# Laying out the order of a decoder layer's token mixers on five engines by a list of events with operation times

## The chip, the core and the metric

The kernel runs on one core of a Trainium2 chip. A core has five engines that each work through a list of their own, in its order: TensorE (PE in the profile; PEld is its loading of weights), VectorE (DVE), ScalarE (ACT), GpSimd (POOL) and SyncE (SP, which here only issues DMAs). [...] The metric is the device time of the whole program in microseconds (us), the median of several runs; less is better.

## The reference

The program computes one layer for 512 positions of 2048 channels, in float32. What matters here:

```python
h = rms_norm(x, pre_gain[l]) * (1.0 + scale) + shift      # scale, shift, gate from c
proj = h @ w_in[l]                                        # 97 column tiles of 128
y_a = rwkv7_mix(pa, ...)                                  # r, k, v, a low-rank w and a
y_a = (y_a * jax.nn.silu(z_a)) @ p_a[l]
y_b = (short_conv_mix(pb, conv_w[l]) * jax.nn.silu(z_b)) @ p_b[l]
m = jax.nn.sigmoid(g_a) * y_a + jax.nn.sigmoid(g_b) * y_b
o = m @ w_out[l]
x = x + gate * rms_norm(o, post_gain[l])
```

`rwkv7_mix` holds a recurrence over the positions for 16 heads of 64 channels (`S = S*w + sa*b + v*k`, `y = S@r`), followed by a normalisation of y in each head. `short_conv_mix` is a convolution of width 3 along the positions.

## The kernel before, in words

Every float32 product is made of three matmuls: a weight tile `w` is cut into `H` (a rounded copy, made by ACT) and `L = w - H` (made by POOL; `split`, lines 151 to 153), and the inputs likewise; then H·H, H·L and L·H are added in PSUM (`three`, lines 163 to 166). One column tile of the input projection is 16 blocks deep and so takes 48 matmuls of 128x512. Its weights come in four quarters of 256 KB (`quarter`, line 155: a DMA to `raw`, then `wH` on ACT and `wL` on POOL, four buffers of each).

The program has three stages. The first normalises x, makes the modulation and begins the projection (tiles `firsts`). The second, which the change is about, is the mixers' stage. The third multiplies by `p_b`, `p_a` and `w_out`.

In the mixers' stage PE has two kinds of work. One is the **dense stream**: 83 column tiles `ps_c` (79 whole ones, 4 of half depth), 3888 matmuls of 128x512 in all, each tile evicted from one of two PSUM banks (`mm`) by a function of its own (`use_rkv`, `use_za`, `use_gate` and the four of the convolution). The other is the recurrence, worked out for eight pairs of heads in chunks of 64 positions, by three generators a pair:

- `prepare` (line 523): the operands AR and BK of a pair, with its decays, from the tiles of r, k and v; mostly DVE.
- `invert` (line 629): the triangular matrices of all chunks (`pg`, `GG`), then their inversion on DVE, 62 short operations one after another (`invt`, `Xg`, lines 667 and 669), between DMAs that rearrange the blocks.
- `chunks` (line 708): transposes (`pt`, `pv`, `pz`) and then the **chain** of eight chunks. In each, PE makes `p1 = GK·VB + AR·S` (lines 753 and 755), ACT copies it to `UB` in two halves (757), PE makes `p2 = Kt·VB + S + Z·UB` (760, 762, 764), and ACT copies that to the next state `SB` in two halves (767). `p1` and `p2` hold four chunks in one bank each; `p2` has one bank alone (`py=1` in BANKS). After four chunks their sum goes to `yt`: ACT copies p1 (771) and DVE adds p2 (772). At a pair's end DVE normalises yt and writes it to a block-diagonal `YB` (788), PE turns it back with 8 products by `twoid` (793), ACT scales it (795), POOL adds the bonus (796), DVE gates it (801).

What sets the order: for PE alone it is written out. `drive` (line 177) takes the dense stream three matmuls at a time (`STEP = 0.66`) and goes to a generator when the wait that it last asked for (`WAIT`, in us, lines 34 and 35) has gone by on a clock that `drive` counts up. ACT, DVE, POOL and SP are ordered by the framework's scheduler, by priorities (`URGENT` for the chain) and its own estimates.

Of the kernel before, what the change touches and what calls it, by code (L numbers as in the profile page):

```python
# [8 lines left out]
F32 = mybir.dt.float32  # L9
# [7 lines left out]
P = 128  # L17
# [59 lines left out]
def trunk(ctx: ExitStack, tc: tile.TileContext, xT_d, x_d, prm_d, crow_d, ada1_d, ada2_d, rows_d, w_d, lora_d, pa_d, pb_d,  # L77
# [47 lines left out]

    twoid = cst.tile([P, C], F32, name="twoid")
    V.tensor_copy(twoid[0:C, :], ident[0:C, 0:C])
    V.tensor_copy(twoid[C:P, :], ident[C:P, C:P])
# [48 lines left out]
    def drive(stream, sides):  # L177

        now = 0.0
        with tc.manual_schedule(engines={mybir.EngineType.PE}):
            while stream or sides:
                for sd in list(sides):
                    while sd in sides and sd[1] <= now:
                        try:
                            with tc.high_priority(offset=sd[2]):
                                cost, wait = next(sd[0])
                        except StopIteration:
                            sides.remove(sd)  # L190
                            break
                        if cost == wait == 0:
                            break
                        now += cost
                        sd[1] = now + wait
                if stream:
                    try:
                        next(stream)
                    except StopIteration:
                        stream = None  # L200
                now += STEP

# [21 lines left out]
    hold = {}  # L224

    def use_cg(i, ps):
        cg = ev.tile([P, T], F32, tag="cv", bufs=1, name=f"cg{i}")
        A.activation(cg, ps, AF.Copy)
        hold["cg", i] = cg

    def use_hb(i, ps):
        u = ev.tile([P, T], F32, tag="u", bufs=1, name=f"u{i}")
        V.tensor_tensor(u, ps, hold.pop(("cg", i)), ALU.mult)
        v = ev.tile([P, T], F32, tag="cv", bufs=1, name=f"cv{i}")
        A.activation(v, u, AF.Copy, scale=pc("cw", 16 + i))
# [12 lines left out]
    USES = ((T_CG, use_cg), (T_HB, use_hb), (T_BG, use_bg), (T_ZB, use_zb))
# [224 lines left out]
    with tc.tile_pool(name="rp", bufs=1) as rp:  # L473
# [7 lines left out]
        def within(ps, w, H, L):  # L481

            TE.matmul(ps, w, H, start=True, stop=False)
            TE.matmul(ps, w, L, start=False, stop=True)

        def lerp(dst, ps, i):

            m = ev.tile([P, T], F32, tag="th", bufs=1, name=f"lm{i}")
            A.activation(m, ps, AF.Copy, scale=pc("mu", i))
            V.scalar_tensor_tensor(dst[:, 1:T], ps[:, 1:T], omu[:, i:i + 1], m[:, 0:T - 1], ALU.mult, ALU.add)  # L490
            V.tensor_scalar(dst[:, 0:1], ps[:, 0:1], omu[:, i:i + 1], None, ALU.mult)
# [3 lines left out]
        G.memset(keep, 1.0)  # L495
        G.memset(keep[:, :, 0:1], 0.0)


        la = tmp("la")
        lerp(la, first[T_LORA], T_LORA)  # L500
        A.activation(la[0:HS, :], la[0:HS, :], AF.Tanh)
        twin = tmp("twin")
        S.dma_start(twin[HS:P, :], la[0:HS, :])
        S.dma_start(twin[0:HS, :], la[HS:P, :])
# [4 lines left out]
        halves = (slice(0, HS), slice(HS, P))  # L509
        for i, b in enumerate(halves):  # L510
            A.activation(laH[i][b, :], la[b, :], AF.Copy)
            G.tensor_tensor(laL[b, :], la[b, :], laH[i][b, :].bitcast(F32), ALU.subtract)
            A.activation(wz[halves[1 - i], i], ident[halves[1 - i], :], AF.Copy, scale=0.0)
            A.activation(laH[i][halves[1 - i], :], twin[halves[1 - i], :], AF.Copy)
# [5 lines left out]
        def small(name):  # L520
            return bank("sm", f"ps_{name}")

        def prepare(j, got, out):

            n = f"_{j}"
            wa = rp.tile([P, 2, P], F32R, tag="wa", name="wa" + n)
            raw = tmp("raw" + n).rearrange("p (a b c) -> p a b c", a=2, b=2)
            S.dma_start(raw[:, 0], lora_d[j])
            for i, b in enumerate(halves):
                o = halves[1 - i]  # L530
                A.activation(wa[b, i], raw[b, 0, i], AF.Copy)
                A.activation(wz[b, i], raw[b, 0, i], AF.Copy)
                A.activation(raw[o, 1, i].bitcast(F32R), raw[o, 0, i], AF.Copy)
                G.tensor_tensor(wa[o, i], raw[o, 0, i], raw[o, 1, i], ALU.subtract)
            yield 0, WAIT["w"]
            psw = small("w" + n)
            lowrank(psw, wa[:, 0], 0)
            lw = tmp("lw" + n)
            A.activation(lw, psw, AF.Tanh, bias=hw0[:, j:j + 1], scale=0.5)
            V.tensor_scalar(lw, lw, -0.5 * DECAY, -0.5 * DECAY, ALU.mult, ALU.add)  # L540
            cum3 = c3(lw)
            for t0 in range(0, T, T // 4):
                part = lw[:, t0:t0 + T // 4]
                V.tensor_tensor_scan(part, keep.rearrange("p c t -> p (c t)"), part, 0.0, ALU.mult, ALU.add)
            dec = rp.tile([P, NC, C + 1], F32, tag="dec", name="dec" + n)
            G.memset(dec[:, :, 0:1], 1.0)
            A.activation(dec[:, :, 1:C + 1], cum3, AF.Exp)
            A.activation(lw, lw, AF.Exp, scale=-1.0)
            end = rp.tile([P, NC], F32, tag="end", bufs=2, name="end" + n)
            A.activation(end.unsqueeze(2), dec[:, :, C:C + 1], AF.Copy)  # L550
            yield 0.5, WAIT["a"]
            psa = small("a" + n)
            lowrank(psa, wa[:, 1], 1)
            a = tmp("a" + n)
            A.activation(a, psa, AF.Tanh, bias=hw0[:, 8 + j:9 + j], scale=0.5)
            V.tensor_scalar(a, a, 0.5, 0.5, ALU.mult, ALU.add)
            while "k" not in got:
                yield 0, 0
            kr = got["k"]
            sq = tmp("sq" + n)  # L560
            A.activation(sq, kr, AF.Square, scale=pc("kk", j))
            sH, sL = tmp("sH" + n, F32R), tmp("sL" + n, F32R)
            split(sH, sL, sq)
            yield 0.5, WAIT["k"]

            psk = small("k" + n)
            within(psk, hsumr, sH, sL)
            V.tensor_scalar(sq, psk, 1e-24, None, ALU.max)
            kk = tmp("kk" + n)
            rsqrt(kk, sq, tmp("ku" + n))  # L570
            V.scalar_tensor_tensor(kk, kr, pc("kk", j), kk, ALU.mult, ALU.mult)
            u = tmp("u" + n)
            G.tensor_scalar(u, a, pc("ka", j), oka[:, j:j + 1], ALU.mult, ALU.add)
            V.tensor_tensor(kr, kr, u, ALU.mult)
            yield 0.5, WAIT["kk"]
            while "r" not in got or at["chain"] < j - 1:
                yield 0, 0
            rr, vv = got["r"], got["v"]


            AR = rp.tile([P, NC, P], F32, tag="AR", bufs=2, name="AR" + n)
            BK = blocks_of(j)
            V.tensor_tensor(a, kk, a, ALU.mult)
            for h, b in enumerate(halves):
# [564 lines left out]
```

## Time and profile before

| what | before |
|---|---|
| median of 3 runs (lowest, highest) | 1716.77 us (1715.26, 1724.05) |
| the profiled execution's own time | 1715.66 us |
| its span, first to last instruction | 1713.9 us |
| mean granted TensorE clock | 0.980 |
| PE busy in the span | 1631.9 us, 95% |
| DVE, ACT, POOL busy | 51%, 38%, 47% |
| first and last dense matmul of the mixers' stage | 192.9 us, 1327.1 us |
| DMA, mean | 138 GB/s |

The profile is of one execution. "Busy" of PE counts a matmul from its start to a modelled end, and matmuls overlap; a gap in it is a true wait, though, and the tables of waits name the instruction that waited, what ended the wait and how long it took. The granted clock is the share of full speed that the throttle allowed TensorE; at 0.5 each matmul takes twice as long.

### The profile page before, as it was taken

How to read it: one execution, taken by the hardware profiler on the slowest of the kernel's cores; microseconds unless marked ns; L12 is line 12 of the kernel's file. 1: busy time of each engine (PE TensorE's matmuls, PEld its weight loads, DVE VectorE, ACT ScalarE, POOL GpSimd, SP SyncE). 2: the span in 40 equal slices, each digit the busy share in tenths (PEclk: the TensorE clock that was granted, in tenths of full speed). 3: DMA queues.
4: the chain of work that ended last, by engine and by line, in shares of the span. 5: the costliest groups of instructions: out<-in, count | busy, mean ns of one | idle time of the engine just before them, and what ended most of it. 6: DMA issues, size and time to landing. Idle time of an engine off the chain costs nothing. (4 is left out here: it accounts for less than half of the span.)

```text
span 1713.9 us, 22888 instructions
## 1 busy us (share of the span) xinstructions
PE 1631.9 (95%) x8120; PEld 1345.5 (79%) x8120; DVE 875.3 (51%) x1582; ACT 644.0 (38%) x1331; POOL 805.0 (47%) x649
## 2 busy tenths in 40 slices
PE   6999989999998999998999989999999899999997
PEld 3788877787887887887878878878887687888886
DVE  4997778319629438448168076152002344544405
ACT  4554522344353343443433433433432323232411
POOL 2699653533533534444435434334344344774421
PEclk8999999999999999999999999999999899999999
DMA  8985332323332432322323324343333676665704
GB/s 321 363 330 203 108 103 74 114 78 97 90 90 64 123 83 79 108 83 85 121 84 104 98 75 122 92 119 113 97 105 102 228 240 209 195 197 182 242 32 148
DMA packets 138885, 235.71 MB, mean 138 GB/s; under 512 B 34833, under 2 KB 43665, under 8 KB 134673
## 3 DMA queue, kind: packets, MB, share of 16 engines
q1 hardware_dynamic: 138624, 234.15, 43.3%
q8 instruction: 64, 1.05, 0.2%
q14 instruction: 51, 0.42, 0.1%
q10 hardware_dynamic: 146, 0.09, 0.0%
HBM read 214.79 MB, written 19.14 MB: 136 GB/s over the span
## 5 line engine op out<-in xcount | busy, mean ns | idle before, releaser
L153 POOL TENSOR_TENSOR wL_c<-raw_c,wH_c 128x512 fp32r<-128x512 f32 x324 | 435.1, 1346 | 564.5 <-ACT wH_c L152 562.0
L164 PE MATMUL ps_c<-hH,wH_c 128*128 128x512 f32 x1296 | 531.1, 410 | 5.7 <-DVE firsts L836 2.3
L166 PE MATMUL ps_c<-hH,wL_c 128*128 128x512 f32 x1296 | 511.2, 394 | 2.9 <-POOL wL_c L153 2.9
L165 PE MATMUL ps_c<-hL,wH_c 128*128 128x512 f32 x1296 | 510.4, 394 | 0.0
L152 ACT ACTIVATE wH_c<-raw_c 128x512 fp32r<-128x512 f32 x324 | 203.3, 630 | 421.1 <-PE ps_c L165 182.8
L166 PEld LDWEIGHTS ps_c<-hH,wL_c 128*128 128x128 f32 x1296 | 246.0, 190 | 58.3 <-POOL wL_c L153 4.5
L164 PEld LDWEIGHTS ps_c<-hH,wH_c 128*128 128x128 f32 x1296 | 247.3, 191 | 52.9 <-ACT wH_c L152 2.9
L165 PEld LDWEIGHTS ps_c<-hL,wH_c 128*128 128x128 f32 x1296 | 247.4, 191 | 44.7
L153 POOL TENSOR_TENSOR fL<-fraw,fH 128x512 fp32r<-128x512 f32 x56 | 79.9, 1435 | 50.6 <-ACT fH L152 50.4
L669 DVE TENSOR_TENSOR Xg<-Xg,invt 128x60 f32<-128x60 f32 (+24 forms) x248 | 97.4, 393 | 6.5
L153 POOL TENSOR_TENSOR oL<-wo,oH 128x512 fp32r<-128x512 f32 x48 | 65.4, 1369 | 61.6 <-ACT oH L152 60.1
L164 PE MATMUL fps<-hH,fH 128*128 128x512 f32 x224 | 88.8, 396 | 3.7 <-ACT hH L322 3.7
L667 DVE TENSOR_TENSOR invt<-M,Xg 128x60 f32<-128x60 f32 (+24 forms) x248 | 82.5, 333 | 16.6 <-DMA M<-s 10.1
L165 PE MATMUL fps<-hL,fH 128*128 128x512 f32 x224 | 88.7, 396 | 1.9 <-DVE hL L325 1.9
L166 PE MATMUL fps<-hH,fL 128*128 128x512 f32 x224 | 88.3, 394 | 1.7 <-POOL fL L153 1.7
L801 DVE SCALAR_TENSOR_TENSOR za<-y,za 128x512 f32<-128x512 f32 x8 | 5.5, 692 | 155.8 <-POOL y L796 155.8
L641 DVE TENSOR_TENSOR GG<-pg,gmask 128x512 f32<-128x512 f32 x32 | 22.1, 691 | 123.0 <-PE pg L640 122.9
L308 DVE SCALAR_TENSOR_TENSOR ada<-ada,csr 128x2048 f32<-128x2048 f32 x32 | 72.6, 2276 | 9.8 <-PE csr L336 9.8
L165 PE MATMUL po<-oL,mH 128*128 128x512 f32 x192 | 74.9, 390 | 0.2 <-POOL oL L153 0.2
L166 PE MATMUL po<-oH,mL 128*128 128x512 f32 x192 | 74.7, 389 | 0.0
L164 PE MATMUL po<-oH,mH 128*128 128x512 f32 x192 | 74.7, 389 | 0.0
L772 DVE TENSOR_TENSOR yt<-p,yt 64x256 f32<-64x256 f32 x32 | 13.5, 422 | 105.5 <-PE p L764 59.1
(282 smaller groups left out, 2657.7 us busy)
## 6 DMA issues: line engine op xcount, KB each, us to landing
raw_c<-in_w_dram SPq DMA_DIRECT2D x324, 256.0 KB, 2.6
ada<-in_ada_dram SPq DMA_DIRECT2D x32, 1024.0 KB, 9.3
gr<-in_ada_dram SPq DMA_DIRECT2D x64, 256.0 KB, 4.4
wo<-in_wo_dram SPq DMA_DIRECT2D x64, 256.0 KB, 3.8
fraw<-in_w_dram SPq DMA_DIRECT2D x56, 256.0 KB, 4.6
raw_pb<-in_pb_dram SPq DMA_DIRECT2D x32, 256.0 KB, 2.7
raw_pa<-in_pa_dram SPq DMA_DIRECT2D x32, 256.0 KB, 2.7
th_s<-th SPq DMA_DIRECT2D x30, 256.0 KB, 2.0
```

What stands on the lines that cost most here:

```text
L152: A.activation(H, src, AF.Copy)
L153: eng.tensor_tensor(L, src, H.bitcast(F32), ALU.subtract)
L164: TE.matmul(ps, wH, xH, start=start, stop=False)
L165: TE.matmul(ps, wH, xL, start=False, stop=False)
L166: TE.matmul(ps, wL, xH, start=False, stop=stop)
L308: V.scalar_tensor_tensor(ada[j, i], ada[j, i], 0.5, csr, ALU.mult, ALU.mult, accum_out=accs[j][:, i:i + 1])
L641: V.tensor_tensor(g[:, c0:c0 + 4, :], pg, gmask.unsqueeze(1).to_broadcast([P, 4, P]), ALU.mult)
L667: V.tensor_tensor(w, TT[:, s, s + 1:HB].unsqueeze(2).to_broadcast([P, m, u]), Xg[:, s, 0:u].unsqueeze(1).to_broadcast([P, m, u]), ALU.mult)
L669: V.tensor_tensor(Xg[:, s + 1:HB, 0:u], Xg[:, s + 1:HB, 0:u], w, ALU.add)
L772: V.tensor_tensor(yt[o, c - 3:c + 1, :], p2[o, :, b], yt[o, c - 3:c + 1, :], ALU.add)
L801: V.scalar_tensor_tensor(z, y, 0.5, z, ALU.mult, ALU.mult)
```

## The change

The first and the third stage stay as they are. In the mixers' stage all five engines now have a written order (`manual_schedule(engines=ALL)`). A list of generators is stepped on one counted clock `now`:

- Each operation on ACT, DVE or POOL is placed by `run(engine, cost, ...)` with a duration of its own. `run` keeps the time until which each engine is busy, places an operation only when its engine's backlog is at most `SOON = 1.2` us, and returns when the result is ready (`HOP = 0.2` later). Operations of DVE with two operands in SBUF and all of POOL (`DVE2`, `POOL`) exclude each other in that account.
- A generator yields the time at which it can go on (`t + SURE`, `now + SUM`) in place of a fixed wait. So the chain's steps follow on the readiness of UB and SB.
- `fetch` accounts a DMA by its size, `take` a PSUM bank by the time of its eviction.
- `loader`, `high` and `low` load and cut the quarters of the next column tile while one tile is at work; `dense` gives one matmul at a time, in a slightly other order of column tiles.
- The preparation of pair j starts at (j-1)·106 us of that clock at the earliest (`PACE`).
- Some work is another: ACT now copies p2 too, to `y2` (the other half of the room VY), and DVE adds yt and y2 once a pair; the normalised yt is turned back by 16 products of 64x64 in the array's two off-diagonal corners in place of the 8 full ones by `twoid`; `evac_z` works in its own output and not in a shared `th`; `end` has three buffers in place of two; memsets of the stage's rooms are placed in `zeros`.

In the changed kernel nearly all operations of ACT, DVE and POOL in this stage carry the line of `run`'s call (428), so there they are told apart by tile.

The middle of a pair's chain, after its fourth chunk, on DVE before: pair 3's inversion, with the sum of pair 2 (`yt_2`) in it.

```order
L669 TENSOR_TENSOR Xg_3_5584<-Xg_3_5584,invt_3_23_5659 128x8x6
L667 TENSOR_TENSOR invt_3_24_5662<-M_3_5579,Xg_3_5584 128x49
L669 TENSOR_TENSOR Xg_3_5584<-Xg_3_5584,invt_3_24_5662 128x7x7
L772 TENSOR_TENSOR yt_2_5510<-p2_2_0_5512,yt_2_5510 64x256 x2
L667 TENSOR_TENSOR invt_3_25_5665<-M_3_5579,Xg_3_5584 128x42
L669 TENSOR_TENSOR Xg_3_5584<-Xg_3_5584,invt_3_25_5665 128x6x7
```

The same place on ACT now: behind the state's copy (`SB`) stand the four copies that empty p1 and p2 of pair 2.

```order
L428 ACTIVATE UB_1769<-p1_2_0_5757 64x64 x2
L428 ACTIVATE wH_c12_3_5914<-raw_c12_3_5786 128x512
L428 ACTIVATE yb7_5924<-ps_c64_5753 128x512
L428 ACTIVATE a_4_5928<-ps_a_4_5906,hw0_96 128x512
L428 ACTIVATE SB_1768<-p2_2_0_5758,end_2_3900 64x64 x2
L428 ACTIVATE VY_3422<-p1_2_0_5757 64x256
L428 ACTIVATE VY_3422<-p2_2_0_5758 64x256
L428 ACTIVATE VY_3422<-p1_2_0_5757 64x256
L428 ACTIVATE VY_3422<-p2_2_0_5758 64x256
L428 ACTIVATE wH_c20_0_5955<-raw_c20_0_5916 128x512
```

So p2's bank is emptied by ACT, and DVE has no part in it. The one addition of yt and y2 (`VY<-VY 128x512`) stands on DVE after the last step of pair 3's inversion.

One chunk of pair 2 on PE before, from p1 to the next dense matmul behind `Z·UB` (names: ps_c is the dense stream):

```order
L753 MATMUL p1_2_0_5511<-VY_3174,GG0_1787 128x128
L755 MATMUL p1_2_0_5511<-SB_1789,AR_2_4005 128x128
L760 MATMUL p2_2_0_5512<-VY_3174,ZK_3176 128x128
L762 MATMUL p2_2_0_5512<-SB_1789,ident_77 128x128
L164 MATMUL ps_c20_5828<-hH2_442,wH_c20_0_5831 128x512
...
L166 MATMUL ps_c20_5828<-hH5_700,wL_c20_1_5868 128x512
L764 MATMUL p2_2_0_5512<-UB_1790,ZK_3176 128x128
L164 MATMUL ps_c20_5828<-hH6_762,wH_c20_1_5867 128x512
```

And a chunk of pair 2 now:

```order
L877 MATMUL p1_2_0_5757<-VY_3422,GG0_1766 128x128
L879 MATMUL p1_2_0_5757<-SB_1768,AR_2_4357 128x128
L883 MATMUL p2_2_0_5758<-VY_3422,ZK_3436 128x128
L885 MATMUL p2_2_0_5758<-SB_1768,ident_77 128x128
L1036 MATMUL ps_c64_5753<-hH11_1231,wH_c64_2_5708 128x512
...
L1036 MATMUL ps_c64_5753<-hH12_1299,wL_c64_3_5764 128x512
L890 MATMUL p2_2_0_5758<-UB_1769,ZK_3436 128x128
L1036 MATMUL ps_c64_5753<-hH13_1371,wH_c64_3_5751 128x512
```

Between p1 and `Z·UB` 12 dense matmuls stood before and 6 stand now; between `Z·UB` and the next p1 mostly 21 stood and 9 stand. The four chunks' break has 15 there now, in pair 2.

The end of the stage on SP before: the loads of the finished convolution tiles for the third stage (`yb`).

```order
L157 DMA raw_pb3_0_11896<-in_pb_dram 128x512
L848 DMA th_s_1756<-th29_11602 128x512
L157 DMA raw_pb3_1_11914<-in_pb_dram 128x512
L932 DMA yb0_11718<-yb_s_114 128x512
L932 DMA yb1_11722<-yb_s_114 128x512
```

And now:

```order
L443 DMA th_s_1753<-th22_11120 128x512
L443 DMA raw_c75_3_11156<-in_w_dram 128x512
L1129 DMA yb0_11747<-yb_s_111 128x512
L1129 DMA yb1_11751<-yb_s_111 128x512
L443 DMA raw_c76_0_11213<-in_w_dram 128x512
```

They moved from behind the stage's last store (th29) to seven stores ahead of it. On PE the last product of pair 7 (`y_7`) stood behind the last dense matmul of the stage and directly ahead of the third stage's first product; it now stands behind the third matmul of column tile c74, with 333 dense matmuls after it.

The core of the diff (the kernel's generators are wrapped in `run`, `take` and `yield` throughout):

```diff
-WAIT = dict(w=9.41, a=1.49, k=5.88, kk=8.64, g0=9.5, g=2.2, inv=80.0, p=2.0, y=2.0, t=1.3, z=1.3, u=2.0,
-            s=4.4, n=25.0, b=12.0, b2=6.0)
-STEP = 0.66
-URGENT = 3000
+HOP, SURE, SOON, SUM = 0.2, 0.6, 1.2, 0.35
+PACE = 106.0
...
-        with tc.manual_schedule(engines={mybir.EngineType.PE}):
...
+    with tc.tile_pool(name="rp", bufs=1) as rp, tc.manual_schedule(engines=ALL):
+        now = 0.0
+        busy, port = dict(DVE=0.0, ACT=0.0, POOL=0.0, DMA=0.0), []
+        def run(eng, cost, f, *args, **kw):
+            two = eng in ("POOL", "DVE2")
+            e = eng[:3] if eng == "DVE2" else eng
+            while busy[e] > now + SOON:
+                yield busy[e] - SOON
+            f(*args, **kw)
+            t = max(now, busy[e])
+            if two:
+                while port and port[0][1] <= now:
+                    port.pop(0)
+                for b, c in port:
+                    if b < t + cost and t < c:
+                        t = c
+                port.append((t, t + cost))
+                port.sort()
+            busy[e] = t + cost
+            return busy[e] + HOP
+        def fetch(size, out, src, fixed=1.9):
+            S.dma_start(out, src)
+            begin = max(now, busy["DMA"])
+            busy["DMA"] = begin + size / 300.0
+            return busy["DMA"] + fixed
+        def take(tag, name, n=T):
+            while books[tag][0][0] is None or books[tag][0][0] > now:
+                yield now + 0.25 if books[tag][0][0] is None else books[tag][0][0]
...
-                for b in halves:
-                    A.activation(UB[b, b], o1[b, b], AF.Copy)
-                yield 0.9, WAIT["u"]
+                for b in halves:
+                    t = yield from run("ACT", 0.22, A.activation, UB[b, b], o1[b, b], AF.Copy)
+                yield t + SURE
                 TE.matmul(o2, Z[:, c, :], UB, start=(c == NC - 1), stop=True)
...
-                        V.tensor_tensor(yt[o, c - 3:c + 1, :], p2[o, :, b], yt[o, c - 3:c + 1, :], ALU.add)
-                yield 0.22, WAIT["s"]
+                        b2[0] = yield from run("ACT", 0.38, A.activation, y2[o, c - 3:c + 1, :], p2[o, :, b], AF.Copy)
+                yield t + SURE
...
-                TE.matmul(yps[:, c * C:(c + 1) * C], YB[:, c, :], twoid, start=True, stop=True)
+                for b, o in zip(halves, halves[::-1]):
+                    TE.matmul(yps[b, c * C:(c + 1) * C], yt[o, c, :], ident[o, o], start=True, stop=True,
+                              tile_position=(o.start, b.start))
...
+        def dense():
...
+                        for w, x in ((H, hH), (H, hL), (L, hH)):
+                            TE.matmul(ps, w[:, i, :], x[k], start=(k == k0 and x is hH and w is H),
+                                      stop=(k == KT - 1 and w is L))
+                            spend(0.227)
...
+        sides = [[g, 0.0] for g in (
+            high(), low(), loader(), uses(soon), uses(due),
+            side("chunks", lambda j: "solved" in ops[j] and "bon" in ops[j], lambda j: chunks(j, **ops[j])),
+            side("ops", paced, lambda j: prepare(j, rkv[j], ops[j])),
+            side("inv", lambda j: at["made"] > j, lambda j: invert(j, out=ops[j], **ops[j])),
+            zeros())]
```

More of the change, by code (lines that the diff above doesn't have):

```diff
@@ L495, in trunk @@
[L495 to L504, printed above, removed]
+            t = yield from run("ACT", 0.68, A.activation, m, ps, AF.Copy, scale=pc("mu", i))
+            yield t
+            yield from run("DVE", 0.72, V.scalar_tensor_tensor, dst[:, 1:T], ps[:, 1:T], omu[:, i:i + 1], m[:, 0:T - 1],
+                           ALU.mult, ALU.add)
@@ L508, in trunk @@
         wz = rp.tile([P, 2, P], F32R, name="wz")
[L509 to L514, printed above, removed]
+        BKs = [rp.tile([P, NC, 2, P], F32, name="BK0"), None]
@@ new lines, in trunk, with zeros @@
+        GG = rp.tile([P, 2, NC, P], F32, name="GG0")
+        XB = rp.tile([P, NC, P], F32, name="XB")
+        SB = rp.tile([P, 2, P], F32, name="SB")
+        UB = rp.tile([P, P], F32, name="UB")
+        rooms = {}
+        def zeros():
+            yield from run("POOL", 0.2, G.memset, keep, 1.0)
+            yield from run("POOL", 0.2, G.memset, keep[:, :, 0:1], 0.0)
+            for z, t in ((BKs[0], 1.9), (XB, 1.0), (SB, 0.3), (UB, 0.2)):
+                yield from run("POOL", t, G.memset, z, 0.0)
+            at["zeros"] = 1
@@ L518, in lowrank @@
             TE.matmul(ps, wz[:, i], laL, start=False, stop=True)
-        def small(name):
-            return bank("sm", f"ps_{name}")
+            spend(0.46)
         def prepare(j, got, out):
@@ L545, in prepare @@
+            a = tmp("a" + n)
+            book[0] = yield from run("ACT", 0.69, A.activation, a, psa, AF.Tanh, bias=hw0[:, 8 + j:9 + j], scale=0.5)
             dec = rp.tile([P, NC, C + 1], F32, tag="dec", name="dec" + n)
[L546 to L556, printed above, removed]
+            yield from run("POOL", 0.12, G.memset, dec[:, :, 0:1], 1.0)
+            yield t
+            yield from run("ACT", 0.63, A.activation, dec[:, :, 1:C + 1], cum3, AF.Exp)
+            yield from run("ACT", 0.63, A.activation, lw, lw, AF.Exp, scale=-1.0)
@@ L557, in prepare @@
+            end = rp.tile([P, NC], F32, tag="end", bufs=3, name="end" + n)
+            yield from run("ACT", 0.22, A.activation, end.unsqueeze(2), dec[:, :, C:C + 1], AF.Copy)
+            yield from run("DVE", 0.55, V.tensor_scalar, a, a, 0.5, 0.5, ALU.mult, ALU.add)
             while "k" not in got:
-                yield 0, 0
+                yield now + 0.3
             kr = got["k"]
             sq = tmp("sq" + n)
-            A.activation(sq, kr, AF.Square, scale=pc("kk", j))
             sH, sL = tmp("sH" + n, F32R), tmp("sL" + n, F32R)
-            split(sH, sL, sq)
@@ L564, in prepare @@
[L564 to L568, printed above, removed]
+            yield from run("ACT", 0.72, A.activation, sq, kr, AF.Square, scale=pc("kk", j))
+            yield (yield from run("ACT", 0.63, A.activation, sH, sq, AF.Copy))
+            yield SURE + (yield from run("POOL", 1.3, G.tensor_tensor, sL, sq, sH.bitcast(F32), ALU.subtract))
+            psk, book = yield from take("sm", "ps_k" + n)
@@ L687, in lower @@
+            yield l3 + HOP
+            for h in range(NH):
+                t = fetch(32, part(1, h), s3[h * NC:(h + 1) * NC, 1].rearrange("q j t -> j q t"))
+            yield t + SURE
+            def lower(name, left, right, out):
+                ps, books = [], []
+                for h in range(NH):
+                    p, book = yield from take("pg", f"{name}{h}{n}", NC * HB)
+                    ps.append(p.rearrange("p (c t) -> p c t", c=NC))
+                    books.append(book)
                 for c in range(NC):
@@ L785, in chunks @@
[L785 to L793 removed]
+            yield b2[0]
+            yield from run("DVE2", 0.7, V.tensor_tensor, yt, yt, y2, ALU.add)
```

611 lines of the change are left out of this document (371 added, 240 removed).

## The prediction

> **What bounds the kernel now.** The page's head first, then the busy time by stretch: the mixers' stage cut at its start and end, and the third stage.
>
> ```profile
> span 1713.9 us, 22888 instructions
> 193.00:330.00 137.00, 125.17 (x545) 101.14 (x544) 100.27 (x172) 43.79 (x83) 67.39 (x55) 0.98 0.34 97
> 330.00:1300.00 970.00, 939.57 (x5142) 790.43 (x5141) 464.73 (x984) 381.73 (x845) 406.96 (x331) 0.98 0.33 97
> 1300.00:1341.00 41.00, 32.20 (x131) 24.29 (x130) 5.18 (x10) 12.47 (x21) 13.41 (x11) 0.88 0.43 140
> ```
>
> The columns are the stretch, its length, PE, PEld, DVE, ACT and POOL busy, and the granted clock. PE is the engine that is nearly always at work; DVE, ACT and POOL have room to spare. So the stage can only gain what PE idles in it, 11.8 + 30.4 + 8.8 = 51.0 us, and what the clock lost beside that. Next, who PE waited for: the stage's middle, its start, its end.
>
> ```profile
> PE p L760 <- DVE invt L667: 11.5, 3, 6.2
> PE p L760 <- DVE Xg L669: 9.5, 3, 4.3
> PE p L760 <- DVE yt L772: 5.3, 1, 5.3
> PE p L764 <- ACT UB L757: 2.5, 2, 1.9
> PE ps_k L484 <- POOL sL L153: 1.6, 2, 1.0
> PE ps_c L166 <- POOL wL_c L153: 2.9, 3, 1.3
> PE pg L640 <- DVE BK L587: 2.7, 1, 2.7
> PE ps_c L164 <- DVE firsts L836: 2.3, 1, 2.3
> PE py_b L164 <- ACT bH L152: 6.3, 1, 6.3
> ```
>
> The columns are the sum, the number and the longest. One place carries the middle: seven waits of L760, once for seven of the eight pairs, 11.5 + 9.5 + 5.3 = 26.3 us. The timeline of the longest, at pair 2, shows what it is.
>
> ```profile
> 770.61 0.39 PE L755 MATMUL p<-SB,AR 128*128 128x128 f32 x2
> 770.79 1.29 DVE L667 TENSOR_TENSOR invt<-M,Xg 128x75 f32<-128x75 f32 x1
> 772.49 0.68 DVE L146 TENSOR_TENSOR ku<-kk 128x512 f32<-128x512 f32 x1
> 776.17 0.86 DVE L772 TENSOR_TENSOR yt<-p,yt 64x256 f32<-64x256 f32 x2
> 777.17 0.76 PE L760 MATMUL p<-VY,ZK 128*128 128x128 f32 x2 [6.17 <-DVE invt L667]
> ```
>
> L760 opens p2 for the second four chunks, in its only bank; the bank is free when DVE has added p2 to yt (L772); and DVE, which works in order, has that addition among the steps of the next pair's inversion and of a preparation (ku). The dense matmuls behind L760 wait too.
>
> Third, the clock after those waits.
>
> ```profile
> 405.00:415.00 10.00, 7.65 (x32) 6.29 (x31) 9.38 (x24) 2.13 (x7) 4.25 (x4) 0.83 0.21 54
> 525.00:537.00 12.00, 7.73 (x33) 6.28 (x32) 11.82 (x32) 2.16 (x7) 2.58 (x2) 0.86 0.24 68
> 645.00:660.00 15.00, 11.72 (x44) 9.44 (x44) 14.37 (x36) 4.72 (x13) 6.49 (x6) 0.77 0.20 54
> 768.00:783.00 15.00, 8.82 (x36) 7.29 (x35) 14.85 (x38) 2.11 (x6) 3.01 (x3) 0.77 0.13 37
> 1010.00:1025.00 15.00, 9.68 (x39) 7.96 (x38) 14.96 (x36) 1.86 (x5) 3.39 (x3) 0.77 0.14 44
> 1135.00:1145.00 10.00, 7.92 (x33) 6.44 (x32) 9.14 (x26) 2.92 (x7) 2.56 (x2) 0.83 0.15 52
> ```
>
> Six of the seven waits are followed by a spell of lower clock. Its loss is length times what is missing from 1: 1.7 + 1.7 + 3.45 + 3.45 + 3.45 + 1.7 = 15.4 us.
>
> **The change, term by term.** The sum is made against the profiled execution, 1715.66 us (span 1713.9 and 1.8 around it), 1.1 us under the runs' median of 1716.77.
>
> *The bank of p2.* ACT empties it in place of DVE. Of the seven waits nothing is left that DVE could cause. What is late next is ACT: behind the state's copy come four copies, two of them on p2, as long as those that ACT made of p1 before.
>
> ```profile
> L771 ACT ACTIVATE yt<-p 64x256 f32<-64x256 f32 x32 | 12.0, 374 | 2.0 <-PE ps_k L484 1.7
> 743.71 0.39 PE L164 MATMUL ps_c<-hH,wH_c 128*128 128x512 f32 x1
> 745.07 0.38 PE L753 MATMUL p<-VY,GG 128*128 128x128 f32 x2
> 745.29 0.39 PE L755 MATMUL p<-SB,AR 128*128 128x128 f32 x2
> 745.71 0.46 ACT L757 ACTIVATE UB<-p 64x64 f32<-64x64 f32 x2 [2.06 <-PE p L755]
> 748.02 0.38 PE L764 MATMUL p<-UB,ZK 128*128 128x128 f32 x2
> 748.44 0.63 ACT L767 ACTIVATE SB<-p,end 64x64 f32<-64x64 f32 x2 [1.13 <-PE p L764]
> ```
>
> From the start of L764 to the end of SB are 0.42 + 0.63 = 1.05 us, and four copies of 374 ns make 2.55. Dense matmuls follow each other by 0.227 us (six steps in 745.07 - 743.71); the 15 that now stand there last 3.4, with two products of 0.22 (745.29 - 745.07) behind them. So it is covered by over 1 us: gain 26.3, with 15.4 of clock. The 32 more copies, 12 us of ACT, lie in a stage where ACT is busy for 438 of 1148 us and cost nothing by themselves. If one other ACT operation of 0.6 us or so slips in ahead, the cover still holds; with three it doesn't.
>
> *The stage's start.* 11.8 us of waits, and 0.02·137 = 2.7 of clock. The first `pg` stood behind 171 dense matmuls and now behind some 310, so that DVE has 30 us more for BK: the 2.7 us go. The waits for wL_c came from POOL, which stood at a memset of `dec` until the products of the pair before were done; the memset now stands in its own preparation. The waits for `firsts` and the rest hang on DVE, which is busiest in this stretch (100 of 137 us). The memsets that come into this stage fall to POOL, which is idle for half of it. I take two thirds, 10 us; the ends are 0 and 14.5.
>
> *The end.* 8.8 us of waits and 0.12·41 = 4.9 of clock. The timeline there:
>
> ```profile
> 1331.46 0.69 DVE L801 SCALAR_TENSOR_TENSOR za<-y,za 128x512 f32<-128x512 f32 x1 [35.52 <-POOL y L796]
> 1332.18 3.65 SPq L932 DMA_DIRECT2D yb<-yb_s x8
> 1332.18 0.60 ACT L911 ACTIVATE th_a<-pg_a 128x512 f32<-128x512 f32 x1 [2.10 <-DVE za L801]
> 1334.89 0.63 ACT L152 ACTIVATE bH<-yb 128x512 fp32r<-128x512 f32 x1 [2.11 <-DMA yb<-yb_s]
> 1335.56 0.69 DVE L153 TENSOR_TENSOR bL<-yb,bH 128x512 fp32r<-128x512 f32 x1 [3.02 <-ACT bH L152]
> ```
>
> The third stage's tiles get the memory of pair 7's last operands, so `yb` is loaded only after DVE's last gating. With y_7 333 dense matmuls (333·0.227 = 76 us) ahead of the end, the loads are done long before; they are moved past seven stores and the last tiles' weight loads on SP, where DMA is busy for 0.33 to 0.43 of the time, and can delay none of those by more than the 3.65 us that their eight issues take, with a tile of 10.9 us (48 matmuls) loaded ahead. What is late next is ACT: bH stands behind th_a, and th_a needs the last matmul ahead of py_b: 0.60 + 0.63 and then bL 0.69, about 2.2 us with hand-overs, and perhaps half of the clock's loss. Gain 6.5 + 3 = 9.5; ends 4 and 13.7.
>
> *Small ones.* The two waits of ps_k, 1.6 us, go, since a step now waits for POOL's result. The products that turn y back:
>
> ```profile
> 593.24 1.89 PE L793 MATMUL y<-twoid,VY 128*128 128x64 f32 x16
> 591.13 0.69 PE L691 MATMUL pw<-XB,GG 32*32 32x32 f32 x32
> ```
>
> Eight full products (two instructions each) take 1.8 us; 16 of a 32x32 corner 0.7. The new ones, 16 of 64x64, lie between: I take 1.3, and 0.2 for entering and leaving, a gain of 8·0.3 = 2.4. If 16 went like 16 full ones it would cost 8·1.8 = 14.4; if like the small ones, gain 8.8.
>
> *What it costs.* Each hand-over of the chain has less cover. The chunk quoted is one of the few with only 9 dense matmuls there: UB was done at 746.17 and L764 came at 748.02, 1.85 us later; with 6 in place of 9 some 1.2 us is left. After Z·UB 9 dense matmuls and the first product of p1 (2.04 + 0.22) stand against the 1.05 us of SB, which also leaves 1.2. ACT's other work decides:
>
> ```profile
> L152 ACT ACTIVATE wH_c<-raw_c 128x512 fp32r<-128x512 f32 x324 | 203.3, 630 | 421.1 <-PE ps_c L165 182.8 <-issue 135.2 <-POOL wL_c L153 76.0
> ```
>
> One `wH` of 630 ns ahead of a copy is covered, two are not; and behind a copy that is late stand further wH, on which the dense stream waits in its turn. Before, 2 of 64 waits of L764 cost 2.5 us together. If one of eight of the 128 hand-overs loses 0.63 us, that is 16·0.63 = 10 us. The ends are 0, and 0.63 at each, 81.
>
> Sum: 26.3 + 15.4 + 10 + 9.5 + 1.6 + 2.4 - 10 = 55.2, and 1715.7 - 55.2 = 1660.5.
>
> [...]
>
> **The rivals.**
>
> *All of it goes.* No new wait: 51.0 + 15.4 + 2.7 + 4.9 + 2.4 = 76.4, so 1639. For it: the waits name few causes. Against: the shorter cover. 0.12.
>
> *The chain eats half.* Hand-overs lose 0.3 us on average, 38 us in place of 10: 1688. For it: UB stands behind another copy of 0.6 us in many places of the new order. 0.15.
>
> *Only the ends gain.* DVE's backlog is not gone: an inversion step can still last 1.29 us, as the one quoted, and the masks of GG (on DVE) free the pg banks, which transposes and pg now take turns at with 1 to 5 dense matmuls between. If that stops PE for as long as L760 did, 41.7 come back: 1702. Against: no pg wait in the middle of the table above. 0.10.
>
> *The change does little:* ACT's and DVE's written order gives back as much as it takes, within 0.5%. 0.04.
>
> *Slower: short waits bring the clock down.* A chunk now holds 15 dense matmuls and five small ones, 15·0.227 + 5·0.22 = 4.5 us, 64 of them 288 us. If each hand-over loses 0.25 (32 us) and the clock in the chains falls to the 0.77 of the rows above (0.23·288 = 66 us), 98 are lost against 65 gained without the 10: 1749. It decides from about 65 us of loss, a clock of 0.88 in the chains. Against it speaks this row, with 30 - 25.91 = 4.1 us of waits (the three for wL_c, of at most 1.3 us, among them) at full clock:
>
> ```profile
> 280.00:310.00 30.00, 25.91 (x111) 20.19 (x110) 29.22 (x62) 5.98 (x14) 10.70 (x11) 1.00 0.17 49
> ```
>
> [...] 0.07.
>
> **How the numbers follow.** The forecast with its own spread (1648 to 1676) has 0.52. A measurement of this kernel can tell about 0.5% (8.6 us) from no change. Faster: 0.52 + 0.12 + 0.15 + 0.08 of "only the ends" = 0.87. Within 0.5%: 0.04 + 0.02 = 0.06. Slower: 0.07. The range reaches from 1638 (all of it goes) to 1703 (only the ends), which leaves out the slower case and no change.
>
> **What would show it.** Right: no wait of the product that opens p2 (now L883); PE's idle time from 193 us to the third stage at 20 us or so, in many waits under 1 us for UB and SB; a granted clock of 0.99 there; bH's wait at 2 us; the third stage as long as before. Wrong: waits of PE for DVE of several us in the chain, waits for UB and SB that sum to over 30 us, or dips of the clock in the chains without a long wait ahead.

## The result, and the profile after

| | before | after |
|---|---|---|
| median of the runs on one chip (lowest, highest) | 1716.51 us (1715.26, 1724.05) | 1642.53 us (1641.22, 1647.3) |
| the profiled execution's own time, span | 1715.66, 1713.9 us | 1647.3, 1645.0 us |
| PE busy, share of the span | 1631.9 us, 95% | 1610.1 us, 98% |
| DVE, ACT, POOL busy | 51%, 38%, 47% | 54%, 40%, 49% |

The ratio is 0.9565 with a 95% interval of 0.9532 to 0.9599: 74 us faster, where 55 were forecast.

How long the mixers' stage lasts is read from two rows of each kernel, the first dense matmul and the first product of `p_b`; behind the colon stand the least, median and greatest duration in ns, then the first and last start. Before:

```profile
L164 PE MATMUL ps_c<-hH,wH_c x1296: 387/389/774, 193.1 to 1326.7; 128*128 128x512 f32 x186
...
L164 PE MATMUL py_b<-bH,wH_pb x128: 388/389/792, 1335.6 to 1425.6; 128*128 128x512 f32 x128
```

After:

```profile
L1036 PE MATMUL ps_c<-hH,wH_c x1296: 387/389/501, 199.3 to 1255.9; 128*128 128x512 f32 x186
...
L160 PE MATMUL py_b<-bH,wH_pb x128: 389/389/499, 1269.2 to 1357.5; 128*128 128x512 f32 x128
```

The stage went from 1335.6 - 193.1 = 1142.5 us to 1269.2 - 199.3 = 1069.9, so 72.6 us of the gain lie in it; the third stage behind it went from 1713.9 - 1335.6 = 378.3 to 1645.0 - 1269.2 = 375.8. (The profiled execution of the changed kernel begins the stage 6.2 us later than the one before did, in the unchanged first stage; it is also the longest of its four runs.) Below, "the stage" is always this length. Its busy time by stretch, after:

```profile
193.00:330.00 137.00, 135.71 (x612) 111.96 (x611) 103.68 (x155) 55.02 (x101) 78.78 (x67) 1.00 0.35 107
330.00:1240.00 910.00, 909.91 (x5225) 763.28 (x5224) 490.00 (x991) 391.11 (x878) 407.62 (x332) 1.00 0.35 105
1240.00:1270.00 30.00, 28.36 (x124) 22.82 (x122) 0.85 (x2) 9.81 (x17) 14.21 (x11) 1.00 0.37 114
```

PE (second number) is busy for all but 1.29 + 0.09 + 1.64 = 3.0 us, against 51.0 us before, and the granted clock (third from the right) is 1.00 in all three. Who PE still waits for, with the sum, the number and the longest:

```profile
PE py_b L160 <- ACT bH L148: 1.5, 1, 1.5
PE py_b L161 <- DVE bL L149: 0.8, 2, 0.6
PE ps_c L1036 <- POOL wL_c L428: 0.6, 1, 0.6
PE ps_a L625 <- ACT lw L428: 0.6, 1, 0.6
```

No wait of the product that opens p2 (L883), none for UB or SB. How a hand-over looks now, in a chunk where two long operations of ACT stand ahead of UB (timeline after):

```profile
650.48 0.63 ACT L428 ACTIVATE wH_c<-raw_c 128x512 fp32r<-128x512 f32 x1 [0.80 <-issue]
651.14 0.69 ACT L428 ACTIVATE lm<-ps_c,prm 128x512 f32<-128x512 f32 x1
651.15 0.39 PE L879 MATMUL p<-SB,AR 128*128 128x128 f32 x2
...
651.73 0.45 ACT L428 ACTIVATE UB<-p 64x64 f32<-64x64 f32 x2
...
653.21 0.38 PE L890 MATMUL p<-UB,ZK 128*128 128x128 f32 x2
```

p1 is done at 651.54, UB is copied from 651.73 to 652.18, and Z·UB comes at 653.21: 1.03 us are left, though the list put a `wH` and an eviction there.

### The profile page after: what moved, and what is told of

Same layout as the page of the kernel before. It is cut to its first block, busy times and chain, and to the rows that moved or that the text cites. A ratio compares the mean times of both kernels' runs of the same rounds, so it can differ in the third digit from the quotient of the medians.

```text
span 1645.0 us, 23157 instructions
## 1 busy us (share of the span) xinstructions
PE 1610.1 (98%) x8248; PEld 1325.5 (81%) x8248; DVE 887.9 (54%) x1548; ACT 654.5 (40%) x1363; POOL 808.7 (49%) x649
## 5 line engine op out<-in xcount | busy, mean ns | idle before, releaser
L1036 PE MATMUL ps_c<-hH,wH_c 128*128 128x512 f32 x1296 | 512.8, 396 | 0.0
L1036 PEld LDWEIGHTS ps_c<-hH,wH_c 128*128 128x128 f32 x1296 | 243.7, 188 | 47.7
L1036 PEld LDWEIGHTS ps_c<-hL,wH_c 128*128 128x128 f32 x1296 | 243.7, 188 | 46.7
L428 DVE TENSOR_TENSOR invt<-M,Xg 128x60 f32<-128x60 f32 (+24 forms) x248 | 87.2, 351 | 42.3 <-DMA M<-s 34.6
L428 DVE TENSOR_TENSOR Xg<-Xg,invt 128x60 f32<-128x60 f32 (+24 forms) x248 | 83.9, 338 | 8.0
L245 DVE SCALAR_TENSOR_TENSOR ada<-ada,csr 128x2048 f32<-128x2048 f32 x32 | 72.6, 2276 | 13.9 <-PE csr L273 13.9
L148 ACT ACTIVATE oH<-wo 128x512 fp32r<-128x512 f32 x64 | 38.4, 627 | 74.1 <-PE po L162 46.7
L149 POOL TENSOR_TENSOR wL_pb<-raw_pb,wH_pb 128x512 fp32r<-128x512 f32 x32 | 41.3, 1292 | 49.4 <-ACT wH_pb L148 49.4
```

The lines of the kernel that those rows point to most:

```text
L148: A.activation(H, src, AF.Copy)
L149: eng.tensor_tensor(L, src, H.bitcast(F32), ALU.subtract)
L245: V.scalar_tensor_tensor(ada[j, i], ada[j, i], 0.5, csr, ALU.mult, ALU.mult, accum_out=accs[j][:, i:i + 1])
L428: f(*args, **kw)
L1036: TE.matmul(ps, w[:, i, :], x[k], start=(k == k0 and x is hH and w is H), stop=(k == KT - 1 and w is L))
```

## The experiments

The theory with which the experiments began is the prediction's: DVE's addition of p2 made the seven waits, so taking p2's bank from DVE brings the middle's gain. Its rival: it is not who empties the bank, but that all engines follow one list that counts their times. When the runs spoke for the rival, it was split further, by engine. Each ratio is against the kernel before on the same chip; the stage is that of the one profiled execution.

| run | median, us | ratio, 95% interval | the stage, us |
|---|---|---|---|
| before + ACT copies p2 | 1734.4 | 1.0085 (1.0065 to 1.0104) | 1158.8 |
| before + the new way of y | 1731.31 | 1.0048 (1.0030 to 1.0066) | 1153.6 |
| after, DVE adds p2 again | 1642.57 | 0.9559 (0.9529 to 0.9588) | 1069.7 |
| after, written order on PE alone | 1721.4 | 1.0012 (0.9994 to 1.0029) | 1147.5 |
| after, on PE and ACT | 1707.68 | 0.9908 (0.9886 to 0.9930) | 1126.2 |
| after, on PE and DVE | 1648.31 | 0.9572 (0.9547 to 0.9598) | 1071.7 |
| after, on PE, ACT and DVE | 1652.08 | 0.9583 (0.9561 to 0.9604) | 1071.9 |
| before, DVE's order written too | 1815.74 | 1.0559 (1.0517 to 1.0602) | 1237.8 |
| after, SURE 0 | 1648.7 | 0.9580 (0.9552 to 0.9607) | 1073.4 |
| after, SURE -1 | 1682.26 | 0.9792 (0.9753 to 0.9831) | 1106.3 |
| after, y_7 last | 1645.75 | 0.9569 (0.9542 to 0.9595) | 1071.1 |
| after, longer groups | 1643.23 | 0.9563 (0.9525 to 0.9600) | 1069.3 |

### Who empties p2's bank

**Before, with ACT copying p2**, into a tile of its own:

```diff
-                        V.tensor_tensor(yt[o, c - 3:c + 1, :], p2[o, :, b], yt[o, c - 3:c + 1, :], ALU.add)
+                        A.activation(y2[o, c - 3:c + 1, :], p2[o, :, b], AF.Copy)
...
+            V.tensor_tensor(yt, yt, y2, ALU.add)
```

> The kernel before with one part of the change alone: ACT copies p2 to a tile y2 and DVE adds yt and y2 once a pair; nothing else is moved by hand. Theory 1 (the engine that empties p2's bank made the seven waits): the waits of L760 and the six dips of the clock behind them go, 26.3 + 15.4 = 42 us, so about 1675 us, ratio 0.976, granted clock 0.985 or more. Theory 2 (the order made them; any engine without a written order can be late): the waits stay at the same place under ACT's name, at least half of them, 1695 us or more.

It was slower. The longest sum among the waits of PE:

```profile
PE p L761 <- ACT y L773: 22.4, 3, 9.3
```

And what ACT's copy waits for:

```profile
ACT y L773 <- DVE ku L147: 23.9, 3, 8.9
```

The product that opens p2 (now L761) waits as long as before, for ACT's copy, and that copy waits for DVE: y2 took a slot of the temporary pool (`tmp`) that DVE's `ku` still held. So this run says only that DVE's lateness came through a memory slot, and the next one takes y2 from elsewhere.

**Before, with the whole new way of y**: yt and y2 in the two halves of the room VY, one addition a pair, 16 products of 64x64; nothing of the order changed.

```diff
-            VB, YB = room_of("VY", True)
+            VB, yy = room_of("VY", True)
+            yt, y2 = yy[:, 0:NC // 2, :].rearrange("p c (a v) -> p (c a) v", a=2), \
+                yy[:, NC // 2:NC, :].rearrange("p c (a v) -> p (c a) v", a=2)
```

> The kernel before with the whole of the new way of y (ACT copies p2 to a tile of its own, one addition of DVE a pair, 16 products of 64x64), and its old scheduling. Theory 1, DVE's part in emptying p2's bank made the seven waits: they go, 26.3 us and most of the 15.4 us of clock, and y saves 4: 1670 to 1680. Theory 2, the order by readiness made the gain: ACT is placed by the framework's scheduler, so other waits of several us for ACT's copies or for GG take their place, and the time is 1705 to 1735 with a clock below 0.985.

Slower again, by 0.3 to 0.7%. The wait for p2's bank is gone, and others have its length:

```profile
PE p L756 <- ACT SB L768: 16.5, 3, 9.2
PE p L765 <- ACT UB L758: 16.2, 4, 7.8
```

The timeline of the longest:

```profile
805.48 0.75 DVE L591 SCALAR_TENSOR_TENSOR rk<-rk,prm,rk 128x512 f32<-128x512 f32 x1
806.26 0.63 ACT L152 ACTIVATE bH<-rk 128x512 fp32r<-128x512 f32 x1 [14.71 <-DVE rk L591]
...
807.44 0.63 ACT L768 ACTIVATE SB<-p,end 64x64 f32<-64x64 f32 x2
808.12 0.79 PE L756 MATMUL p<-SB,AR 128*128 128x128 f32 x2 [9.24 <-ACT SB L768]
```

ACT works in order. It stood for 14.71 us at the cut of another pair's `rk`, which DVE made late, and the state's copy stood behind it. ACT has taken over the copy and has inherited DVE's lateness with it. So the change of engine without a change of order brings nothing.

**After, with DVE adding p2 again**, placed by the list like every other operation:

```diff
-                        b2[0] = yield from run("ACT", 0.38, A.activation, y2[o, c - 3:c + 1, :], p2[o, :, b], AF.Copy)
+                        yield b1[0]
+                        b2[0] = yield from run("DVE", 0.42, V.tensor_tensor, yt[o, c - 3:c + 1, :], p2[o, :, b],
+                                               yt[o, c - 3:c + 1, :], ALU.add)
```

> The changed kernel with that part undone: DVE adds p2 to yt as before, but at a place that the event list gives it. Theory 1 (the engine): the product that opens p2 waits for DVE once a pair again, 20 to 42 us with the clock, 1663 to 1685 us. Theory 2 (the order): DVE's backlog is at most about 1.2 us and an operation of POOL 1.3 us when the addition is placed, which 10 or more dense matmuls cover: waits of p2 under 5 us in all, 1643 to 1650 us.

The time is that of the changed kernel. DVE's 32 additions, by their group:

```profile
L428 DVE TENSOR_TENSOR VY<-p,VY 64x256 f32<-64x256 f32 x32 | 13.5, 422 | 69.1 <-ACT VY L428 65.9 <-PE ps_k L471 1.7 <-PE p L890 0.8
```

And the stretch of the stage's middle:

```profile
330.00:1240.00 910.00, 910.00 (x5227) 763.58 (x5227) 494.81 (x1009) 382.68 (x848) 409.31 (x331) 1.00 0.37 105
```

DVE empties the bank as it did before the change, and PE is never idle. The first theory has fallen.

### Whose order

The next four run the changed kernel with `manual_schedule(engines=...)` of fewer engines; the others' operations are left to the framework's scheduler. PE's row of instructions stays as the list wrote it.

**On PE alone.**

> The changed kernel with the written order kept on PE alone; ACT, DVE, POOL and SP are ordered by the framework's scheduler from the same program. Theory 1: DVE is out of the chain and PE's order is the same, so PE waits little: under 15 us more, at most 1660 us. Theory 2: the copies of UB, SB and p2 fall behind others on ACT, and masks behind inversion steps on DVE; PE waits 30 us or more, 1675 us or more.

All of the gain is gone. The waits of PE:

```profile
PE y L921 <- DVE VY L428: 18.1, 3, 8.0
PE p L890 <- ACT UB L428: 10.9, 3, 4.4
PE p L879 <- ACT SB L428: 7.3, 2, 4.7
PE pv L848 <- ACT GG L428: 7.1, 1, 7.1
```

**On PE and ACT, on PE and DVE, on PE, ACT and DVE.**

```diff
-    with tc.tile_pool(name="rp", bufs=1) as rp, tc.manual_schedule(engines=ALL):
+    with tc.tile_pool(name="rp", bufs=1) as rp, tc.manual_schedule(engines={mybir.EngineType.PE, mybir.EngineType.DVE}):
```

> The changed kernel with the written order on PE and ACT alone; DVE, POOL and SP by the framework's scheduler. If ACT's order is what PE alone lacked (in the run with PE's order alone, UB, SB, GG and VY by ACT made 30 us of PE's 48 us of waits): the waits for UB, SB and GG go, those for DVE (y, 18 us) stay, 1670 to 1690. If it takes all engines together, DVE is still late by several us in places: 1700 to 1725.

> The changed kernel with the written order on PE and DVE alone; ACT, POOL and SP by the framework's scheduler. If DVE's order is what counts: the waits of y's products for DVE (18 us) go, and GG, which ACT makes from what DVE made, is no longer late; 1670 to 1690. If ACT's counts, UB, SB and GG stay late (30 us and their clock): 1700 to 1720.

> The changed kernel with the written order on PE, ACT and DVE; POOL and SP by the framework's scheduler. If the order of the two engines that the chain goes through is what counts: within 0.3% of the changed kernel, 1643 to 1650. If the loads on SP and the cuts on POOL by the list count too, waits for wL and wH come (POOL and SP late): 1655 to 1700.

The first of these came as its second alternative had it (1700 to 1725), the second faster than either of its two, and the third within 0.3% of the changed kernel by its ratio, as its first. With ACT's order and not DVE's, the waits for UB and SB are nearly gone (1.9 and 1.1 us), and the products that turn y back wait longer:

```profile
PE y L921 <- DVE VY L428: 33.0, 4, 9.9
```

The timeline around the longest of those, on DVE and PE:

```profile
705.90 0.69 DVE L428 TENSOR_TENSOR BK<-a,lw 64x512 f32<-64x512 f32 x1
706.62 0.17 DVE L428 SCALAR_TENSOR_TENSOR st<-st 128x8 f32<-128x8 f32 x1
706.82 0.69 DVE L428 TENSOR_TENSOR BK<-rk,lw 64x512 f32<-64x512 f32 x1
...
708.28 0.68 DVE L428 TENSOR_TENSOR VY<-VY,st 128x512 f32<-128x512 f32 x1
...
709.02 1.97 PE L921 MATMUL y<-ident,VY 64*64 64x64 f32 x32 [9.91 <-DVE VY L428]
```

DVE has no wait here (it is busy for 9.79 of the 10 us from 699 on). The steps that PE waits for, the inverse square root in y's normalisation (`st`, mostly 0.17 us each), alternate with operations of 0.69 us for the next pair, which PE is not waiting for. Of these 10 us some 7 go to such operations; the other 3 are the steps themselves. So most of the wait is the order.

With DVE's order and not ACT's, POOL's or SP's, PE is as full as in the changed kernel:

```profile
193.00:330.00 137.00, 137.00 (x622) 113.95 (x621) 98.83 (x152) 47.17 (x85) 74.04 (x57) 1.00 0.37 106
330.00:1240.00 910.00, 907.27 (x5208) 759.75 (x5207) 481.06 (x985) 390.83 (x877) 404.76 (x329) 1.00 0.37 104
```

The intervals of these two kernels with DVE's order (0.9547 to 0.9598, 0.9561 to 0.9604) overlap that of the changed kernel, and their stages are 2 us longer. So of the written orders DVE's makes the gain, given PE's; that of ACT shortens the stage by 21 us where DVE is late (1147.5 to 1126.2) and by nothing that can be told where it is not; those of POOL and SP bring nothing that can be told (the program, with its loads ahead, is the same in these runs; only their order is left to the scheduler).

**Before, with DVE's order written in the order in which its generators come to their operations**, without durations:

```diff
-        with tc.manual_schedule(engines={mybir.EngineType.PE}):
+        with tc.manual_schedule(engines={mybir.EngineType.PE, mybir.EngineType.DVE}):
```

> The kernel before with DVE's order written too, in the order in which its generators come to their operations, so without durations: a step's operations of DVE stand together, the 62 of an inversion or the nine of a preparation's root in one piece. If any written order of DVE does it (the framework's estimates were the fault): the seven waits go, 1675 to 1690. If the interleaving by durations is what counts: DVE's operations that others wait for stand behind up to 20 us of another pair's, PE waits long and often, and it is slower than before, over 1725.

Slower by 5.2 to 6.0%. The longest sum among PE's waits, and that for p2's bank:

```profile
PE ps_k L483 <- ACT sH L152: 61.3, 4, 17.0
...
PE p L760 <- DVE yt L772: 14.4, 4, 7.2
```

The timeline of the longest of them:

```profile
820.13 0.17 DVE L669 TENSOR_TENSOR Xg<-Xg,invt 128x8 f32<-128x8 f32 x1
...
825.39 0.63 ACT L547 ACTIVATE dec<-lw 128x512 f32<-128x512 f32 x1 [14.55 <-DVE lw L544]
828.00 0.80 PE L483 MATMUL ps_k<-sH,hsumr 128*128 128x512 f32 x1 [16.98 <-ACT sH L152]
```

The last operation of an inversion is at 820.13; the ones before it stand back to back. ACT waits 14.55 us for DVE's `lw`, which stands behind the inversion, and PE 16.98 us for what ACT makes next. That an order is written is not enough: operations that others wait for have to stand between those that can wait.

### The cover of the hand-overs

`SURE` is what a generator adds to the time at which its operand is ready: 0.6 in the change.

> The changed kernel with SURE at 0 in place of 0.6: 3 dense matmuls between p1 and Z·UB in place of 6, and 6 in place of 9 behind it. By the slack read from the changed kernel's trace (Z·UB comes 0.72 us at least after UB, the next product of p1 1.2 us after SB), 0.68 us less leaves it without loss: 1640 to 1645. If a hand-over's cover is as thin as the prediction took it (one in eight loses 0.63 us at six dense matmuls), three fewer cost 10 to 20 us: 1652 to 1662.

> The changed kernel with SURE at -1.0 in place of 0.6: mostly no dense matmul is left between p1 and Z.UB (6 before) and 2 or 3 between Z.UB and the next p1 (9 before). In the changed kernel's trace the hand-overs have 1.17 us (UB) and 1.47 us (SB) to spare in the median; 6 and 7 dense matmuls less are 1.36 and 1.59 us, so that PE waits 0.2 us or so at each of some 120: 25 us. Theory A (short waits cost only themselves): 1660 to 1680 us, clock as in the changed kernel. Rival (short waits bring the clock down): a granted clock clearly under 1 in the chains and 1700 us or more.

With 0 (mostly three dense matmuls between p1 and Z·UB, six behind), the stage is 3.5 us longer; the time, 1648.7, lies between the two that were expected. The weight loads that waited:

```profile
PEld y L921 <- DVE VY L428: 3.9, 4, 1.4
...
PEld p L890 <- ACT UB L428: 1.4, 5, 0.3
```

Only 1.4 us of it are at hand-overs; most of the rest is at y's products. With -1 (mostly no dense matmul between p1 and Z·UB, two or three behind) it is 36.4 us longer:

```profile
PEld p L890 <- ACT UB L428: 21.2, 61, 0.7
PEld p L879 <- ACT SB L428: 6.7, 29, 0.2
```

And the stage's middle:

```profile
330.00:1240.00 910.00, 898.61 (x5049) 742.34 (x5048) 474.81 (x983) 381.48 (x863) 386.44 (x318) 1.00 0.34 97
```

Of the 128 hand-overs 90 now wait, 28 us in all, and the granted clock stays at 1.00: these short waits cost no clock. They account for 28 of the 36.4 us; where the rest went was not followed. (PE's busy time shows only 11.4 us of idling because a dense matmul is drawn 0.39 us long while the next can start 0.23 us after it: about 0.16 us of each wait, an estimate from these two figures, lies under the matmul before.) The time, 1682, is just over what was expected if short waits cost only themselves.

### The end of the stage

Pair 7's chain was held back until fewer than three gate tiles were left, so that y_7 stands behind the last dense matmul again:

```diff
-            side("chunks", lambda j: "solved" in ops[j] and "bon" in ops[j], lambda j: chunks(j, **ops[j])),
+            side("chunks", lambda j: "solved" in ops[j] and "bon" in ops[j] and (j < NP - 1 or len(waiting) < 3),
+                 lambda j: chunks(j, **ops[j])),
```

> The changed kernel with pair 7's chain held back until fewer than three gate tiles are left, so that its y_7 stands behind the last dense matmul of the stage, as before the change. If the place of y_7 made the gain at the stage's end: waits of py_b's first matmuls for bH of 6 us and others of 2 to 3 us come back with a dip of the clock, 8 to 14 us more than the changed kernel: 1651 to 1657. If the loads of the finished tiles are hidden anyway, or other work set the end: under 3 us more, 1642 to 1646.

The stage is 1.2 us longer, and the waits at its end are:

```profile
PE py_b L160 <- ACT bH L148: 1.5, 1, 1.5
PE y L921 <- DVE VY L428: 1.1, 1, 1.1
```

The time is that of the second alternative (1642 to 1646), and the timelines say why. Of before, then of this run:

```profile
1321.71 0.39 PE L166 MATMUL pg_a<-hH,wL_ga 128*128 128x512 f32 x1
...
1327.38 1.89 PE L793 MATMUL y<-twoid,VY 128*128 128x64 f32 x16
...
1335.58 0.79 PE L164 MATMUL py_b<-bH,wH_pb 128*128 128x512 f32 x1 [6.31 <-ACT bH L152]
```

```profile
1251.78 1.15 PE L921 MATMUL y<-ident,VY 64*64 64x64 f32 x32 [1.15 <-DVE VY L428]
...
1252.86 0.50 PE L160 MATMUL pg_a<-hH,wH_ga 128*128 128x512 f32 x1
...
1263.66 0.39 PE L162 MATMUL pg_a<-hH,wL_ga 128*128 128x512 f32 x1
1265.60 0.73 PE L160 MATMUL py_b<-bH,wH_pb 128*128 128x512 f32 x2 [1.55 <-ACT bH L148]
```

Before, the third stage's first tile `pg_a` was spread among the last dense matmuls and was over at 1321.71, so that behind y_7 PE had nothing left but py_b. Now its 48 matmuls stand behind y_7 and last from 1252.86 to 1263.66: they cover gating, loads and cut. With `pg_a` there, it matters by only 1.2 us where y_7 stands, with 333 dense matmuls behind it or none. An early y_7 with `pg_a` spread as before was not run, so the runs don't tell whether that alone would have done as well.

### A version to beat both

PE is full after the change, so only its own work is left. In this version pg, pt, pv and pz take both of their banks at once: 237 groups of small products between dense ones in place of 257.

```diff
-                    pg, book = yield from take("pg", f"pg{n}_{c0}_{i}")
+                    pgs.append((yield from take("pg", f"pg{n}_{c0}_{i}")))
+                for c0, (pg, book) in zip((0, 4), pgs):
                     for k in range(4):
...
```

> The changed kernel with the small products of a preparation in longer groups (pg, pt, pv and pz take both of their banks at once: 237 groups of small products between dense ones in place of 257). PE is full here, so only its own work is left to gain: entering and leaving a group costs about 0.2 us, 20 of them 4 us: 1637 to 1640. If a bank that is awaited longer makes new waits, they eat it: 1643 or more.

The stage is 1069.3 us against 1069.7 and 1069.9 of the two kernels with 257 groups, and the time cannot be told from that of the changed kernel: no gain, and no new wait. This version doesn't beat the changed kernel.

## Why the prediction was right in sign and short in size

The direction, the range and what would be seen were right: no wait of L883, full clock, bH's wait short. Of the 20 us or so of idling that were to be left, only 3.0 are. The forecast of 1660.5 lies 18 us above the median, and the rival "All of it goes" (1639, chance 0.12) lies 3.5 below it: that rival came nearest.

- **"The bank of p2. ACT empties it in place of DVE."** This step failed as a cause. Its size came out about right (seven waits and their six dips are gone), but that is luck as far as its reason goes: the change brought DVE's new order along with ACT's copies. DVE empties the bank just as well when the list places its operations, and ACT empties it without gain when DVE's own order is not written. The wait of L760 named the operation at which DVE was late, not the reason: DVE's backlog of operations for other pairs ahead of it. With the framework's order the same lateness showed at `ku`'s slot, at SB and UB, at GG and at y, wherever PE's written order met DVE next.
- **The stage's start.** 10 of 14.5 taken. PE's idle time there fell from 11.8 to 1.3 us and the clock rose from 0.98 to 1.00, which the prediction priced at 2.7: 13.2. The caution, that DVE is busiest there, was wrong for the same reason: with PE and DVE in written order PE is busy for 137.00 of 137.
- **The end.** 9.5 taken, as 6.5 of waits and 3 of clock. 8.8 us of waits became 1.64, a gain of 7.2. The clock's loss was not 4.9: the row in the prediction includes time in which PE waited, where a low clock costs nothing. What was lost lies behind the stage, at the start of the third:

```profile
1335.60:1341.00 5.40, 5.40 (x12) 4.00 (x13) 4.15 (x7) 3.81 (x7) 0.00 (x0) 0.50 1.03 354
```

That is 0.50·5.40 = 2.7, and it makes up the 2.5 us by which the third stage is shorter. So the term was right, 9.9 for 9.5, though the clock's part of it doesn't come in every execution (see the last section). ACT's part, about 2.2 us left with bL, was right too. Its reason, the place of y_7, was not needed: with pg_a's 48 matmuls behind it, y_7 at the very end costs only 1.2 us.
- **y's products.** 2.4 taken; a block went from 1.89 us to 1.15, so about 8·0.74 = 5.9 at most: the 0.2 us for entering and leaving, which the starts around a block show (last section), are not in it.
- **"If one of eight of the 128 hand-overs loses 0.63 us."** This term of -10 was mis-sized, and with it the forecast was kept from the rival: nothing is lost. Three dense matmuls fewer lose 1.4 us at hand-overs in all, six or seven fewer 28.
- **The sum.** 51.0 - 3.0 = 48.0 of waits, 15.4 + 2.7 = 18.1 of clock and 5.9 make 72.0; the stage shows 72.6. The 5.9 is an upper bound, and so is the clock's 18.1, since a low clock during a wait costs nothing: from 774.70 to 777.10, for one, the clock is 0.50 and PE is busy for 0.00 of 2.40 us. So 0.6 us and somewhat more stay open.
- **The rivals.** "Only the ends gain" rested on DVE's backlog staying: it does so without DVE's written order (33 us at y's products), and not with it. "Short waits bring the clock down" did not happen even with 90 of them, at a clock of 1.00.

What stays open: whether the list's gain on DVE comes from its durations or from when it places an operation. The order without either was slower, but the list was not run with all durations equal. Open, too, is whether PE's new order is needed: alone it brings nothing, but every run with the gain has it.

## What to carry to other kernels

Where one engine's order is written by hand, try giving the engine that it meets most the same list: a wait named after one operation can be the backlog of its whole engine, and moving that operation to another engine then only moves the wait. Before pricing such a move, look at what stands ahead of the late operation, and whether anybody waits for that. And when an end is priced, list every instruction between the last product and the one that waits, since work of the next stage may be what covers it.

## What the runs showed of the hardware

**Leaving the dense stream cost 0.2 us at tiles of 32x32 and 64x64, and nothing that shows at 128x128.** Dense matmuls follow each other by 0.227 us. Around a block of y (64x64, after, 526.80 to 528.54 us) the last dense matmul starts 0.32 us ahead of the block, and the first behind it 0.34 us ahead of the next: 0.2 us more in all. Around the 32x32 products `pw` before (590.81 to 592.09) it is the same. Four products of `pg` (128x128, after, 272.85 to 274.20) take 1.35 us with the dense matmuls ahead of and behind them, and 4·0.22 + 2·0.227 = 1.33. The 20 groups that the version with longer groups saves are of 128x128. They moved the stage by 0.4 to 0.6 us, not by the 4 that 0.2 us a group would have made.

**The same pause was followed by half the clock in one run and by the full clock in another.** The wait of py_b for bH is 1.55 us in several runs. Behind it, in the run with y_7 last and then in the changed kernel:

```profile
1266.80:1270.20 3.40, 3.40 (x9) 2.60 (x8) 2.64 (x5) 1.35 (x3) 0.00 (x0) 0.51 0.56 143
```

```profile
1270.40:1273.80 3.40, 3.40 (x16) 2.81 (x15) 2.62 (x5) 2.40 (x6) 0.37 (x1) 1.00 0.26 82
```

The clock is 0.51 for 3.4 us in one, with 9 matmuls, and 1.00 in the other, with 16, after the same pause. So the length of this one pause does not settle the clock; what does was not shown. Nor did many short ones lower it: the run with SURE at -1 shows 1.00 in the stage's middle with 90 short waits at its hand-overs.

**At a clock of 0.50 a matmul took 1.9 times as long, not quite twice.** Before, behind the wait of 6.31 us, the products of py_b start 0.43 us apart from 1336.89 to 1340.73 us (clock 0.50 from 1335.60 to 1341), and 0.23 us apart from 1341.43 on (clock 0.98 from 1341 to 1346).
